# Half leads: two byte offsets inside one weight unit of an encoder trunk

## The chip, the cores and the metric

The kernel runs on one core of a Trainium2 chip, in one launch. The metric is device time in microseconds. A core has engines that run side by side: TensorE (PE in the profile, with its weight loads as PEld), VectorE (DVE), ScalarE (ACT), GpSimd (POOL) and SyncE (SP, which issues the DMAs here).

## The reference

Two layers of a hybrid encoder over 256 positions of width 1024, float32. Each layer has a token-mixing part with four branches in parallel and a feed-forward part. Cut to what matters:

```python
for l in range(DEPTH):                                   # DEPTH = 2
    h = rms_norm(x, norm_mix_pre[l])
    proj = h @ w_in[l]                                   # 1024 -> all branch inputs and gates
    (c_q, c_kv, k_rope, sc_b, sc_c, sc_x, cf_a, cf_g, gm_u, gm_v, gate_logits) = split(proj)
    y_a, y_b, y_c, y_d = ...                             # attention, short conv, Conformer conv, gMLP, each @ its w_o
    g = sigmoid(gate_logits + gate_b[l])
    merged = g0 * y_a + g1 * y_b + g2 * y_c + g3 * y_d
    x = x + rms_norm(merged @ w_out[l], norm_mix_post[l])
    h2 = rms_norm(x, norm_ffn_pre[l])
    f_g, f_u = split(h2 @ w_ffn_in[l])                   # 1024 -> 2 x 2816
    x = x + rms_norm((silu(f_g) * f_u) @ w_ffn_out[l], norm_ffn_post[l])
```

## The kernel before

All weights of a layer are cut into units of at most 128 x 2048 floats, listed by `unit_list` (line 47) in the order in which they are used. A unit is loaded by one DMA into a `raw` tile (line 341), then split (line 352) into a high part, rounded to the matmul's float32r format by ScalarE, and a low part, the rest, subtracted by VectorE. Both parts stand in one `hl` tile of 2 x 2048 + 64 floats, 65 x 256 bytes a partition; five such tiles rotate. A product of two split operands is three matmuls: high x high, high x low, low x high (`group`, line 398). The activations are split in the same way into `hth` and `htl`, each [128, 2, 8, 128]: token half, eight slices k of the 1024 input columns, and 128 tokens.

This document calls those units that hold all 1024 input rows and 256 output columns full-depth units. The code collects them in `stands` (line 329): 30 a layer, counted here from 0. Units 0 to 5 are used for the Conformer and gMLP inputs, 6 to 11 for the short convolution, 12 to 29 for the feed-forward input (columns 512 and up). `b_unit` (line 549) uses them: the weights are the stationary operand, one 128-column tile at a time, and all 256 tokens move. For each half f of the 256 output columns there are eight slices k with three matmuls each, so a unit is 48 matmuls of 128x256. The stationary tiles of the three are high, high, low of slice k; the moving ones are `hth`, `htl`, `hth`. In the `hl` tile a unit lies with a pitch of 256 columns per slice k; the high part is followed by the low part 2048 floats later.

`phase` (line 332) shifts where a unit begins in its `hl` tile: units that aren't full-depth at 0, full-depth units at 16 floats (64 bytes), and those named in `leads` at 32 floats (128 bytes). `LEADS` (line 37) picks the leads by their number among the 30: 0, 6, 9, 12 and 21. The other 25 are called ordinary units here. Of an offset only what is left modulo 256 bytes is given in this document: 128 for leads and 64 for ordinary units. The change's own words count the distance from the other side, 256 less the offset: 128 for a lead, 192 for an ordinary unit.

The order of work on each engine is planned while the program is built: a small model with a clock (lines 100 to 233) lets TensorE's matmuls advance it and issues pending ScalarE, VectorE and GpSimd work by modelled due times and ranks. Generators (attention, convolution, transposes of the hidden layer) are polled between groups of matmuls (`poll`, line 582) and put their matmuls between those of a unit, so that units 8, 10, 11 and 12 are interrupted by others. The plan goes by modelled times, not by what the chip does.

Of the kernel before, what the change touches and what calls it, by code (L numbers as in the profile page):

```python
# [15 lines left out]
ALU = mybir.AluOpType  # L16
AX = mybir.AxisListType

P = 128
L = 2  # L20
D = 1024
S = 256
T = S // P
KD = D // P
# [9 lines left out]
KG = L * NCOL  # L34
UW = 2048
ROOM = 64
LEADS = (0, 6, 9, 12, 21)
FIRST = 544

O_CQ, O_CKV, O_KR = 0, 256, 512  # L40
# [56 lines left out]
def hybrid_encoder(ctx: ExitStack, tc: tile.TileContext, wts, x_in, pos, invf, cols, rows, wst, out):  # L97
# [129 lines left out]
    def flush(ops):  # L227
        if any(o.left for o in ops):
            urge(ops)
            t = clock[0]  # L230
            while any(o.left for o in ops):
                t += 0.1
                pump(t)
# [28 lines left out]
    act, dve, pool, sp, pe = Engine(nc.scalar, "ACT", cost_act), Engine(nc.vector, "DVE", cost_dve), Engine(nc.gpsimd, "POOL", cost_pool), Engine(nc.sync, "SP", lambda *a: 0.1), Tensor()  # L262
# [14 lines left out]
    def nm(s):  # L277
        cnt[0] += 1
        return f"{s}_{cnt[0]}"
# [30 lines left out]
    def bank(s="pb", hold=False):  # L310
        return psum("pb", s, hold)
# [15 lines left out]
    NU = len(units)  # L327

    stands = [u for u in range(NU) if units[u][2] - units[u][1] == D]
    leads = {stands[k] for k in LEADS}  # L330

    def phase(i):
        u = i % NU
        return (2 if u in leads else 1 if u in stands else 0) * ROOM // 4

    class Weights:
        def __init__(self):
# [14 lines left out]
        def split(self, i):  # L352
            w = widths[i % NU]
            both = wp.tile([P, 2 * UW + ROOM], F32R, tag="hl", name=nm("hl"), bufs=B_HI)
            at0 = phase(i)
            h, lo = both[:, at0 : at0 + UW], both[:, UW + at0 : 2 * UW + at0]
            raw = self.raw.pop(i)
            step = FIRST if i == 0 else 1024
            self.parts[i] = (h, lo)
            spans = [(c, min(w, c + step)) for c in range(0, w, step)]  # L360

            def rank():
                return 0 if i <= self.n + NEAR else 3

            for c, e in spans:
                act.copy(h[:, c:e], raw[:, c:e], rank=rank)
                dve.tensor_tensor(lo[:, c:e], raw[:, c:e], h[:, c:e], op=ALU.subtract, rank=rank, then=self.more if e == w else None)

        def more(self, t=0.0):
            if self.nd < L * NU:  # L370
# [9 lines left out]
        def use(self, n):  # L380
            i = self.n
            self.n += 1
            while i not in self.parts:
                flush(list(pending["DVE"][:1]))
            w = widths[i % NU]
            return tuple(a[:, :w].rearrange("p (k n) -> p k n", n=n) for a in self.parts.pop(i))

        def free(self, n=1):
            self.nf += n
# [8 lines left out]
    def group(o, terms, first=True, last=True):  # L398
        n = len(terms)
        for i, (lh, ll, rh, rl) in enumerate(terms):  # L400
            pe.matmul(o, lh, rh, start=(first and i == 0), stop=False)
            pe.matmul(o, lh, rl, start=False, stop=False)
            pe.matmul(o, ll, rh, start=False, stop=(last and i == n - 1))
            poll()
# [42 lines left out]
    for j in range(2):  # L447
        k = slice(4 * j, 4 * j + 4)
# [46 lines left out]
    hth = cp.tile([P, T, KD, P], F32R, name="hth")  # L495
    htl = cp.tile([P, T, KD, P], F32R, name="htl")

    def pre_norm(t, g):
        h = big()
        ss = small(2)  # L500
        s1 = small(1)
        r = small(1)
        for j in range(2):
            c = slice(512 * j, 512 * (j + 1))
            act.activation(h[:, c], x[:, t, c], AF.Square, scale=D ** -0.5, accum_out=ss[:, j : j + 1], rank=FAST)
            if j == 0:
                pool.tensor_scalar(s1, ss[:, 0:1], EPS, None, op0=ALU.add, rank=FAST)
        rstd_of(r, ss[:, 1:2], s1, rank=FAST)
        if callable(g):
            g = g()  # L510
        for j in range(2):
            c = slice(512 * j, 512 * (j + 1))
            dve.scalar_tensor_tensor(h[:, c], x[:, t, c], r, g[j] if isinstance(g, list) else g[:, c], op0=ALU.mult, op1=ALU.mult, rank=FAST)

        def turn():
            for j in range(2):
                yield need(h)
                b = sbank()
                transposes(b, [h[:, 512 * j + P * k : 512 * j + P * (k + 1)] for k in range(4)])
                bv = b.rearrange("p (k n) -> p k n", n=P)  # L520
                split(hth[:, t, 4 * j : 4 * j + 4, :], htl[:, t, 4 * j : 4 * j + 4, :], bv, FAST)

        return turn()
# [25 lines left out]
    def b_unit():  # L549
        wh, wl = W.use(256)  # L550
        b = bank()
        for f in range(2):
            c = slice(f * P, (f + 1) * P)
            o = b[:, f * S : (f + 1) * S].rearrange("p (t n) -> p t n", n=P)
            group(o, [(wh[:, k, c], wl[:, k, c], hth[:, :, k, :], htl[:, :, k, :]) for k in range(KD)])
        W.free()
        return b

# [23 lines left out]
    def poll():  # L582
        nested[0] += 1
        moved = True
        while moved:
            moved = False
            for w in list(waiting):
                if ready(w):
                    w[2] = next(w[1], None)
                    if w[2] is None:  # L590
                        waiting.remove(w)
                    moved = True
                    break
        nested[0] -= 1
# [16 lines left out]
    def layer(l):  # L611
# [26 lines left out]
        def mla_tr(t, cn):  # L638
            yield need(cn)
            b = sbank()  # L640
            transposes(b, [cn[:, P * k : P * (k + 1)] for k in range(4)])
            for j in range(2):
                o = slice(t * P, (t + 1) * P)
                split(ft2(qc[j])[:, :, o], ft2(ql[j])[:, :, o], b[:, 256 * j : 256 * (j + 1)].rearrange("p (f n) -> p f n", f=2))
# [78 lines left out]
        for j in range(2):  # L723
            b = b_unit()
            th = slot(s="th")
            act.activation(th, b, AF.Tanh, scale=0.5)
            b = b_unit()
            dve.scalar_tensor_tensor(zc[j], th, 1.0, b, op0=ALU.add, op1=ALU.mult)

        def split_op(name, j, src):  # L730
            hi, lo = slot(F32R, name + "h"), slot(F32R, name + "l")
            split(hi, lo, src)
            ops[name][j] = (ft2(hi), ft2(lo))
# [41 lines left out]
        for j in range(2):  # L775
            b = b_unit()
            u = slot(s="gu")
            act.activation(u, b, AF.Gelu_apprx_tanh)
            ug.append(u)
# [433 lines left out]
```

## Time and profile before

| | |
|---|---|
| time, median of 3 runs | 947.82 us (947.7 to 948.02) |
| the profiled execution | 948.06 us |
| its span, first to last instruction | 946.3 us |
| PE busy | 936.9 us, 5888 matmuls |
| DVE, ACT, POOL busy | 670.5, 476.5, 49.0 us |
| mean granted TensorE clock | 0.998 |
| DMA | 179.10 MB, mean 189 GB/s |

The profile is of one execution, whose time stands in the second line. Busy time counts an engine's instructions from start to end; matmuls overlap in the pipeline and their ends are modelled, so the start times of the timeline are the surer reading of TensorE's pace. In timeline rows that merge two matmuls, the start is that of the first. The third matmul of one group and the first of the next both read `hth` and are merged into one row; the middle matmul reads `htl` and has a row of its own in each group.

### The profile page before, as it was taken

The page shows a single profiled execution, that of the slowest core. Times are in us where ns is not written, and L with a number is a line of the kernel's source. Part 1 is how long each engine was busy: PE and PEld are TensorE (multiplying, and loading weights), DVE is VectorE, ACT ScalarE, POOL GpSimd, SP SyncE. Part 2 cuts the span into 40 slices and gives each one's busy share as a digit, 9 for nine tenths or more (in the row PEclk, how much of TensorE's full clock was granted, in tenths as well). Part 3 has the DMA queues.
Part 4 walks back from the last instruction along what each step waited for, and adds up shares of the span by engine and source line. Part 5 has one row for each costly group of instructions (what it writes and reads, how often), then busy time and mean ns, then how long its engine had stood idle before and what let it go on. Part 6 is the DMA issues. An engine that isn't in the chain of part 4 may idle for free.

```text
span 946.3 us, 14540 instructions
## 1 busy us (share of the span) xinstructions
PE 936.9 (99%) x5888; PEld 843.1 (89%) x5888; DVE 670.5 (71%) x1000; ACT 476.5 (50%) x729; POOL 49.0 (5%) x95
## 2 busy tenths in 40 slices
PE   8999999999999999999999999999999999999997
PEld 7899988888888999998899999888888889999885
DVE  6879888898857755554387888788887675555532
ACT  7666745446436644444275656544454454544421
POOL 2200000000002000000041000000000110000000
PEclk9999999999999999999999999999999999999999
DMA  9845354565845655564268244455567366555601
GB/s 349 292 172 178 116 185 149 178 213 189 318 166 178 222 181 201 198 228 178 90 244 291 69 164 164 150 178 195 202 239 265 117 216 235 210 181 185 239 1 44
DMA packets 29875, 179.10 MB, mean 189 GB/s; under 512 B 3824, under 2 KB 3952, under 8 KB 10352
## 3 DMA queue, kind: packets, MB, share of 16 engines
q1 hardware_dynamic: 29664, 178.17, 53.4%
q8 instruction: 46, 0.75, 0.3%
q14 instruction: 21, 0.17, 0.0%
q10 hardware_dynamic: 144, 0.00, 0.0%
HBM read 177.11 MB, written 1.05 MB: 188 GB/s over the span
## 4 chain that ended last, share of the span: by engine, by line
PE 98%; DMA 1%; issue 1%; SPq 0%; ACT 0%; DVE 0%; DVEq 0%; POOLq 0%; POOL 0%
PE pb L256 79%; PE acc L256 12%; PE psd L260 4%; PE psd L256 2%; PE av L256 1%; DMA x<-in_x_dram 1%; SPq L317 0%; ACT h L176 0%; DVE x L176 0%; DVEq L1209 0%; POOLq L1209 0%; ACT hl L176 0%; POOL c L176 0%
## 5 line engine op out<-in xcount | busy, mean ns | idle before, releaser
L176 ACT CAST hl<-raw 128x1024 fp32r<-128x1024 f32 (+4 forms) x321 | 322.2, 1035 | 301.9 <-issue 169.0
L176 DVE TENSOR_TENSOR hl<-raw,hl 128x1024 fp32r<-128x1024 f32 (+4 forms) x321 | 376.7, 1201 | 119.3 <-ACT hl L176 119.3
L256 PE MATMUL pb<-hth,hl 128*128 128x256 f32 x1920 | 334.1, 278 | 0.0
L256 PEld LDWEIGHTS pb<-hth,hl 128*128 128x128 f32 x1920 | 291.6, 188 | 0.4
L256 PE MATMUL pb<-htl,hl 128*128 128x256 f32 x960 | 266.3, 277 | 0.0
L256 PE MATMUL pb<-hl,hth 128*128 128x512 f32 (+1 forms) x832 | 239.5, 379 | 0.4 <-ACT hl L176 0.4
L256 PEld LDWEIGHTS pb<-htl,hl 128*128 128x128 f32 x960 | 180.4, 188 | 0.4
L256 PEld LDWEIGHTS pb<-hl,hth 128*128 128x128 f32 x832 | 147.3, 188 | 26.9 <-ACT hl L176 0.6
L256 PE MATMUL pb<-hl,htl 128*128 128x512 f32 (+1 forms) x416 | 147.4, 375 | 0.2 <-DVE htl L176 0.2
L256 PE MATMUL acc<-hl,fh 128*128 128x512 f32 x352 | 108.5, 389 | 0.0
L176 DVE SCALAR_TENSOR_TENSOR yc<-zc,hcol,yc 128x241 f32<-128x241 f32 (+14 forms) x240 | 97.8, 470 | 0.0
L256 PEld LDWEIGHTS pb<-hl,htl 128*128 128x128 f32 x416 | 74.8, 188 | 14.5 <-DVE htl L176 0.4
L256 PEld LDWEIGHTS acc<-hl,fh 128*128 128x128 f32 x352 | 65.9, 188 | 13.5
L256 PE MATMUL acc<-hl,fl 128*128 128x512 f32 x176 | 68.5, 389 | 0.0
L256 PE MATMUL pb<-hl,mh 128*128 128x512 f32 x128 | 40.0, 394 | 0.0
L256 PEld LDWEIGHTS acc<-hl,fl 128*128 128x128 f32 x176 | 33.0, 188 | 6.8
L176 POOL TENSOR_SCALAR c<-c 128x1 f32<-128x1 f32 (+1 forms) x20 | 12.8, 638 | 503.0 <-ACT sq L176 455.6
L176 DVE TENSOR_TENSOR f<-f,pb 128x512 f32<-128x512 f32 x22 | 15.1, 687 | 30.3 <-PE pb L256 30.3
L176 ACT COPY pt<-psd 128x512 f32<-128x512 f32 x16 | 9.4, 585 | 39.7 <-PE psd L260 39.7
L256 PEld LDWEIGHTS pb<-hl,mh 128*128 128x128 f32 x128 | 23.6, 188 | 4.6
L176 DVE TENSOR_TENSOR h<-acc,gain 128x512 f32<-128x512 f32 x8 | 5.4, 690 | 28.6 <-ACT sq L176 28.5
L256 PE MATMUL pb<-hl,ml 128*128 128x512 f32 x64 | 25.0, 390 | 0.0
(149 smaller groups left out, 837.8 us busy)
## 6 DMA issues: line engine op xcount, KB each, us to landing
raw<-in_wts_dram SPq DMA_DIRECT2D x152, 1024.0 KB, 4.8
brow<-in_rows_dram SPq DMA_DIRECT2D x24, 256.0 KB, 6.0
gain<-in_rows_dram SPq DMA_DIRECT2D x7, 512.0 KB, 5.9
raw<-in_wts_dram SPq DMA_DIRECT2D x3, 816.0 KB, 4.3
raw<-in_wts_dram SPq DMA_DIRECT2D x2, 768.0 KB, 6.7
raw<-in_wts_dram SPq DMA_DIRECT2D x2, 544.0 KB, 5.8
out_dram<-x SPq DMA_DIRECT2D x4, 256.0 KB, 2.1
raw<-in_wts_dram SPq DMA_DIRECT2D x3, 272.0 KB, 4.7
```

What stands on the lines that cost most here:

```text
L176: o.emit = lambda: f(*a, **k)
L256: nc.tensor.matmul(out, lhsT, rhs, **k)
L260: nc.tensor.transpose(out=out, in_=in_, identity=identity)
```

## The change

Placement: `phase` is replaced by `places`, which gives for each unit the places of the first and second 1024 elements of its high part and of its low part in the `hl` tile. For an ordinary unit these are high at 16 and 1040, low at 2064 and 3088 floats (64 bytes modulo 256, as before). For a lead the first 1024 elements are at 2080 (high) and 3104 (low), that is 128 bytes modulo 256, and the second 1024 at 16 and 1040, that is 64 bytes.

Layout: the full-depth units are stored in memory half by half: all eight slices of output columns 0 to 127 first, then those of columns 128 to 255, so that the first 1024 elements are the first half f and the pitch of a slice is 128 columns instead of 256. `b_unit` takes the tiles accordingly. DMAs, copies and subtractions keep their number and sizes.

Leads: 21 is no longer one; 0, 6, 9 and 12 remain.

```diff
--- before.py
+++ after.py
@@ -34,7 +34,7 @@
 KG = L * NCOL
 UW = 2048
 ROOM = 64
-LEADS = (0, 6, 9, 12, 21)
+LEADS = (0, 6, 9, 12)
 FIRST = 544
 
 O_CQ, O_CKV, O_KR = 0, 256, 512
@@ -329,9 +329,11 @@
     stands = [u for u in range(NU) if units[u][2] - units[u][1] == D]
     leads = {stands[k] for k in LEADS}
 
-    def phase(i):
+    def places(i):
         u = i % NU
-        return (2 if u in leads else 1 if u in stands else 0) * ROOM // 4
+        if u in leads:
+            return (2080, 16), (3104, 1040)
+        return ((16, 1040), (2064, 3088)) if u in stands else ((0, 1024), (2048, 3072))
 
     class Weights:
         def __init__(self):
@@ -352,19 +354,18 @@
         def split(self, i):
             w = widths[i % NU]
             both = wp.tile([P, 2 * UW + ROOM], F32R, tag="hl", name=nm("hl"), bufs=B_HI)
-            at0 = phase(i)
-            h, lo = both[:, at0 : at0 + UW], both[:, UW + at0 : 2 * UW + at0]
             raw = self.raw.pop(i)
             step = FIRST if i == 0 else 1024
-            self.parts[i] = (h, lo)
+            self.parts[i] = both
             spans = [(c, min(w, c + step)) for c in range(0, w, step)]
 
             def rank():
                 return 0 if i <= self.n + NEAR else 3
 
             for c, e in spans:
-                act.copy(h[:, c:e], raw[:, c:e], rank=rank)
-                dve.tensor_tensor(lo[:, c:e], raw[:, c:e], h[:, c:e], op=ALU.subtract, rank=rank, then=self.more if e == w else None)
+                hi, lo = (both[:, p[c // 1024] + c % 1024 :][:, : e - c] for p in places(i))
+                act.copy(hi, raw[:, c:e], rank=rank)
+                dve.tensor_tensor(lo, raw[:, c:e], hi, op=ALU.subtract, rank=rank, then=self.more if e == w else None)
 
         def more(self, t=0.0):
             if self.nd < L * NU:
@@ -383,7 +384,10 @@
             while i not in self.parts:
                 flush(list(pending["DVE"][:1]))
             w = widths[i % NU]
-            return tuple(a[:, :w].rearrange("p (k n) -> p k n", n=n) for a in self.parts.pop(i))
+            both = self.parts.pop(i)
+            if i % NU in stands:
+                return tuple(tuple(both[:, o : o + 1024].rearrange("p (k n) -> p k n", n=P) for o in p) for p in places(i))
+            return tuple(both[:, o : o + w].rearrange("p (k n) -> p k n", n=n) for o, _ in places(i))
 
         def free(self, n=1):
             self.nf += n
@@ -550,9 +554,8 @@
         wh, wl = W.use(256)
         b = bank()
         for f in range(2):
-            c = slice(f * P, (f + 1) * P)
             o = b[:, f * S : (f + 1) * S].rearrange("p (t n) -> p t n", n=P)
-            group(o, [(wh[:, k, c], wl[:, k, c], hth[:, :, k, :], htl[:, :, k, :]) for k in range(KD)])
+            group(o, [(wh[f][:, k, :], wl[f][:, k, :], hth[:, :, k, :], htl[:, :, k, :]) for k in range(KD)])
         W.free()
         return b
 
@@ -1170,7 +1173,10 @@
     for l in range(L):
         for name, r0, r1, cols in units:
             w = src[name][l][r0:r1, cols]
-            parts.append(w.reshape(-1, P, w.shape[1]).transpose(1, 0, 2).reshape(-1))
+            w = w.reshape(-1, P, w.shape[1])
+            if r1 - r0 == D:
+                w = w.reshape(KD, P, -1, P).transpose(2, 0, 1, 3).reshape(-1, P, P)
+            parts.append(w.transpose(1, 0, 2).reshape(-1))
     wts = np.concatenate(parts)
 
     def colmajor(v):
```

## Rows read from the trace of the kernel before

**Rows 1.** The page: span, PE's busy time, granted clock in 40 slices.

```profile
span 946.3 us, 14540 instructions
...
PE 936.9 (99%) x5888; PEld 843.1 (89%) x5888; DVE 670.5 (71%) x1000; ACT 476.5 (50%) x729; POOL 49.0 (5%) x95
...
PEclk9999999999999999999999999999999999999999
```

**Rows 2.** The page, part 4: the chain that ended last, by engine.

```profile
PE 98%; DMA 1%; issue 1%; SPq 0%; ACT 0%; DVE 0%; DVEq 0%; POOLq 0%; POOL 0%
```

**Rows 3.** The page, part 5: split copies and 128x256 matmuls (out<-in xcount | busy, mean ns).

```profile
L176 ACT CAST hl<-raw 128x1024 fp32r<-128x1024 f32 (+4 forms) x321 | 322.2, 1035 | 301.9 <-issue 169.0
L176 DVE TENSOR_TENSOR hl<-raw,hl 128x1024 fp32r<-128x1024 f32 (+4 forms) x321 | 376.7, 1201 | 119.3 <-ACT hl L176 119.3
L256 PE MATMUL pb<-hth,hl 128*128 128x256 f32 x1920 | 334.1, 278 | 0.0
...
L256 PE MATMUL pb<-htl,hl 128*128 128x256 f32 x960 | 266.3, 277 | 0.0
```

**Rows 4.** Waits of PE: line, releaser: us in total, times, longest.

```profile
PE pb L256 <- ACT hl L176: 0.4, 1, 0.4
PE pb L256 <- DVE htl L176: 0.2, 1, 0.2
```

**Rows 5.** Timeline of PE (start us, us, what), layer 1, units 6 and 7.

```profile
80.32 0.28 PE L256 MATMUL pb<-htl,hl 128*128 128x256 f32 x1
...
83.20 0.28 PE L256 MATMUL pb<-htl,hl 128*128 128x256 f32 x1
...
86.09 0.28 PE L256 MATMUL pb<-htl,hl 128*128 128x256 f32 x1
...
88.81 0.28 PE L256 MATMUL pb<-htl,hl 128*128 128x256 f32 x1
```

**Rows 6.** Timeline of PE, layer 1, units 20 to 22.

```profile
362.95 0.28 PE L256 MATMUL pb<-htl,hl 128*128 128x256 f32 x1
...
363.29 0.28 PE L256 MATMUL pb<-htl,hl 128*128 128x256 f32 x1
...
363.63 0.28 PE L256 MATMUL pb<-htl,hl 128*128 128x256 f32 x1
...
365.67 0.28 PE L256 MATMUL pb<-htl,hl 128*128 128x256 f32 x1
...
366.02 0.29 PE L256 MATMUL pb<-htl,hl 128*128 128x256 f32 x1
...
368.52 0.28 PE L256 MATMUL pb<-htl,hl 128*128 128x256 f32 x1
...
371.37 0.28 PE L256 MATMUL pb<-htl,hl 128*128 128x256 f32 x1
```

**Rows 7.** Timeline of PE, layer 1, units 12 and 13, and the last of unit 29.

```profile
317.66 0.60 PE L260 MATMUL psd<-ident,f 128*128 128x128 f32 x4
...
322.13 0.28 PE L256 MATMUL pb<-htl,hl 128*128 128x256 f32 x1
...
324.87 0.28 PE L256 MATMUL pb<-htl,hl 128*128 128x256 f32 x1
...
414.55 0.28 PE L256 MATMUL pb<-htl,hl 128*128 128x256 f32 x1
```

**Rows 8.** Timeline of PE, layer 1, units 10 and 11, behind attention work.

```profile
109.07 0.28 PE L256 MATMUL pb<-htl,hl 128*128 128x256 f32 x1
...
111.79 0.28 PE L256 MATMUL pb<-htl,hl 128*128 128x256 f32 x1
...
118.44 0.28 PE L256 MATMUL pb<-htl,hl 128*128 128x256 f32 x1
...
121.26 0.28 PE L256 MATMUL pb<-htl,hl 128*128 128x256 f32 x1
```

## The prediction

> **What bounds the kernel now.** I began with the page's head and its busy shares: TensorE is busy for 936.9 of 946.3 us, at a granted clock in the top tenth in every slice, so it runs at the 2.4 GHz level throughout [rows 1]. The chain that ended last is 98% PE [rows 2]. The waits of PE on the prepared weights come to 0.4 + 0.2 us in the whole run [rows 4]. So a nanosecond saved between two matmuls is a nanosecond of the run, and nothing else can give much. The next thing to read is therefore not who waits, but at what pace matmuls follow each other.
>
> Half of all matmuls belong to the 60 full-depth units: 1920 + 960 = 2880 of 128x256, 48 a unit (two halves of eight groups of three) [rows 3]. The mean of 278 ns in that row hides the pace, since matmuls overlap; the timeline gives it. In each group of three the middle matmul is the only one that reads `htl`, so the start of one `htl` row to the next is one group, and eight groups later is one half unit. Three paces stand there:
> - Ordinary units: 0.34 us a group, 2.72 us a half. Unit 7 of layer 1, 86.09 to 88.81 [rows 5]; unit 20, three successive rows 0.34 apart, and 362.95 to 365.67 [rows 6].
> - Leads: 0.355 to 0.36 us a group. Unit 6 takes 2.88 and 2.89 us for its halves [rows 5], unit 21 takes 2.85 and 2.85 [rows 6]. Of the ten leads three have the 2.88 of unit 6 (units 0 and 6 of layer 1, unit 6 of layer 2), the other seven the 2.85 of unit 21.
> - Some stretches of ordinary units that begin behind other matmuls: 0.353 us a group. Unit 11 of layer 1, 118.44 to 121.26, has 2.82 for eight [rows 8]. Units 10 and 11 of layer 2 are the same.
>
> So an ordinary unit has a fast and a slow pace, 13 ns a group apart, and keeps the one it is in: from 324.87 to 414.55 the feed-forward stage has 263 groups, which at 0.34 make 89.42, and the other 0.26 us are the lead at unit 21 [rows 7]. The trace says what sets the pace: behind a lead, the ordinary unit is fast after about a group (all ten leads); behind an interruption without a lead it is a lottery (unit 10 of layer 1 came out fast, 109.07 to 111.79, the three others slow) [rows 8]. A lead is slower than either pace of an ordinary unit, and what it buys is the fast pace after it. Why a byte offset does this no row shows; I use it as an observed rule.
>
> **The change, part by part.**
>
> *Half a lead instead of a whole one (units 0, 6, 9, 12, both layers: eight leads).* The first 24 matmuls keep offset 128 and their cost. The other 24 get the ordinary offset and, if the fast pace comes, 2.72 us. The three slow leads save 2.88 - 2.72 = 0.16 us each, 0.48; the other five save 2.85 - 2.72 = 0.13 each, 0.65. Together 1.13 us. The switch itself is paid today at the border of the units and then in the middle of one: 322.13 to 324.87 is 2.74, so it costs 0.02 or less [rows 7], and cancels.
>
> *Lead 21 removed.* Units 13 to 29 then have one offset. 365.67 to 371.37 is 5.70 us where two fast halves are 5.44: 0.26 us, with about 0.01 more in the first group after it, so 0.53 for both layers. This needs that the fast pace holds without a second lead for 17 units; today it holds for eight and a half before unit 21 and eight after, with no drift in the rows.
>
> *Weights laid out half by half (256-column pitch to 128).* Copies and subtractions stay at two pieces of 1024 each a unit, 1.04 and 1.20 us [rows 3], the same bytes per DMA, the same order on SP, and no wait is added; each piece is needed no earlier than before (the second 12 matmuls later), so beside PE waits of 0.6 us in all it gives nothing and costs nothing. If this cover were gone (DVE later than PE), 2.4 us of subtraction a unit would still fit into 5.44. What the trace doesn't show is the pace when successive stationary tiles are 512 bytes apart instead of 1024. The ends: every group at the lead's 0.36 costs 60 x 16 x 0.02 = 19 us; every group at 0.34, the fastest that any row of this shape has, would give another 1.13 us in the leads' first halves and 0.6 in the three slow stretches. I take zero, far nearer to the second: today the moving tile steps by 512 bytes per k and the stationary one by 1024, so their offset alternates with even and odd k, and successive groups are still equally 0.34 apart [rows 6]; the buffers are 65 x 256 bytes long, so offsets of 256 alternate from unit to unit as well, and all ordinary units of that stage have the pace. The row nearest to the new case says that only the offset below 256 counts.
>
> *Sum.* 1.13 + 0.53 = 1.66 us, all on the path. The profiled execution took 948.06 us (span 946.3 and 1.8 around it, untouched): 946.40. It lies 0.24 above the median of 947.82, for which the same sum gives 946.16, say **946.2 us, 0.17% less**. About 0.2% (1.9 us) is what a measurement of this kernel can tell from no change, so this counts as "same", though close to the edge.
>
> **The rivals.**
>
> *1. The half lead at unit 12 fails to bring the fast pace (slower).* Today a lead has 48 matmuls behind an interruption, or at unit 12, where four transposes break in at 317.66, 15 before them and 33 after [rows 7]. With half a lead only nine stand between those transposes and the switch. For it to work: unit 21 is at the lead's pace from its first group (365.67 to 366.02 is 0.35) [rows 6], so nine should do. Against: none of the ten switches came so soon after a restart, and a wrong moment costs as unit 11 does. Price: half of unit 12 and 17 units are 280 groups at 2.82/8 - 0.34 = 0.0125 to 0.0133 us, 3.6 us a layer: both layers 953.4, one layer 949.8 (beyond +0.2%). It decides against the change as soon as it happens in one layer. Both layers have the same order of work, so both is likelier: 0.09, against 0.02 for one. The same failure at unit 0 costs 88 groups, 1.2 us, so 947.4 for one layer: 0.03.
>
> *2. The lead's extra time belongs to its place, not its offset (no change).* Being the first of a stage, it would keep its 2.85 in any layout: 947.8. For it: four of five leads do follow other work. Against: unit 21 follows ordinary units without a gap, is slow from its first group to its last, and unit 22 is fast again [rows 6]. 0.04.
> [...]
>
> *3. The fast pace is lost in the long stage without lead 21 (slower).* From unit 21 on, nine units are 144 groups x 0.013 = 1.9 us a layer: 946.2 + 3.8 = 950.0 (two layers). Against: no loss in any row so far, and PE waits for no weights there. 0.03.
>
> *4. The restarts in units 10 and 11 fall differently (faster or nothing).* The change moves the work before them by 0.1 to 0.2 us each, and the state in which the attention's matmuls interrupt. Each of the four stretches has 15 groups, 0.2 us. All fast would give 0.6: 945.6; the one fast one lost gives 946.4. Below 945.9 needs two of the three slow ones to turn. 0.17.
>
> **How the numbers follow.** Forecast 0.62; rival 4 on the fast side 0.17; rival 1 0.14 (0.03 of it within 0.2%); rival 2 0.04; rival 3 0.03. Faster by over 0.2% (below 945.9): 0.17, and 0.02 for the measurement's own spread (947.7 to 948.02 before), 0.19. Slower (above 949.7): 0.09 + 0.02 + 0.03 = 0.14. Same: 0.67. The range runs from all restarts fast, 945.5, to the loss at unit 0 in one layer, 947.5, and leaves out rivals 2, 3 and the large part of 1.
>
> **What would show it.** In the timeline, second halves of units 0, 6, 9 and 12 at 2.72 to 2.74 us, first halves unchanged at 2.85 to 2.89, unit 21 at 2.72 a half, 0.34 a group up to the end of the stage; span 944.6. Wrong if groups of 0.353 follow unit 12 (rival 1), if second halves stay at 2.85 (rival 2), if 0.34 turns to 0.353 in mid-stage (rival 3), or if ordinary units are no longer at 0.34 at all (the layout).

## The result: slower, 953.95 us, and the profile after

The changed kernel takes 953.95 us (953.48 to 954.75) where the kernel before took 947.92 beside it: ratio 1.0064, 95% interval 1.0052 to 1.0076. The forecast of 946.2 and its range (945.5 to 947.5) are missed; the time is that of the first rival on both layers (953.4).

The page of the changed kernel (span; busy us of PE and the other engines):

```profile
span 953.0 us, 14540 instructions
...
PE 944.1 (99%) x5888; PEld 850.8 (89%) x5888; DVE 670.7 (70%) x1000; ACT 476.7 (50%) x729; POOL 47.5 (5%) x95
```

PE's busy time has grown with the span, by 7.2 and 6.7 us, at as many matmuls as before [rows 1]; the granted clock is 0.998 as before. The waits of PE on weights are still next to nothing (releaser: us in total, times, longest), as in [rows 4]:

```profile
PE pb L256 <- DVE htl L176: 0.5, 2, 0.4
```

So the matmuls follow each other more slowly, and the timeline says where. Unit 6 of layer 1 (start us, us, what; `htl` rows are one group of three apart, eight groups make a half):

```profile
80.74 0.28 PE L256 MATMUL pb<-htl,hl 128*128 128x256 f32 x1
...
83.62 0.28 PE L256 MATMUL pb<-htl,hl 128*128 128x256 f32 x1
...
86.34 0.28 PE L256 MATMUL pb<-htl,hl 128*128 128x256 f32 x1
```

The half lead does what it should here: 2.88 us for the first half, 2.72 for the second, which took 2.89 in [rows 5]. The same holds for unit 0 in both layers, unit 6 of layer 2 and unit 9 of layer 1. In the feed-forward stage of layer 1 four transposes break into unit 12. The first row is theirs; the others are the first group of unit 12's second half, the first groups of unit 13's two halves, and the last group of unit 29:

```profile
318.01 0.60 PE L260 MATMUL psd<-ident,f 128*128 128x128 f32 x4
...
319.63 0.28 PE L256 MATMUL pb<-htl,hl 128*128 128x256 f32 x1
...
322.46 0.28 PE L256 MATMUL pb<-htl,hl 128*128 128x256 f32 x1
...
325.28 0.28 PE L256 MATMUL pb<-htl,hl 128*128 128x256 f32 x1
...
418.21 0.28 PE L256 MATMUL pb<-htl,hl 128*128 128x256 f32 x1
```

From 325.28 to 418.21 there are 263 groups in 92.93 us, 0.3533 a group, where [rows 7] have 89.68 with a lead in it. Nothing changes on the way; units 20 and 21, where the lead of before stood, are like all others:

```profile
364.86 0.28 PE L256 MATMUL pb<-htl,hl 128*128 128x256 f32 x1
...
367.68 0.28 PE L256 MATMUL pb<-htl,hl 128*128 128x256 f32 x1
...
370.51 0.28 PE L256 MATMUL pb<-htl,hl 128*128 128x256 f32 x1
...
373.34 0.28 PE L256 MATMUL pb<-htl,hl 128*128 128x256 f32 x1
```

2.82 to 2.83 a half against 2.72 for an ordinary half and 2.85 for a lead in [rows 6]. Layer 2 is the same: 92.93 us over the same 263 groups (793.55 to 886.48). The stage is at the slow pace from the switch in unit 12 to its end, on both layers.

The sum closes. The forecast was -1.66 us. 280 slow groups (half of unit 12 and 17 units) at 0.3533 - 0.34 = 0.0133 us are 3.73 a layer, 7.47 for both; unit 9 of layer 2 switched into the slow pace as well (second half 2.83 instead of 2.72, 0.11) and unit 10 of layer 1 restarted slow (15 groups, 0.20). Together +6.1 us, against 6.03 by the medians. The profiled span grew by 6.7; the other 0.6 us come before unit 0 begins (36.48 against 35.91 for its first `htl` row), in the start-up.

### The profile page after: what moved, and what is told of

Read it like the earlier page. It is cut to its first block, busy times and chain, and to the rows that moved or that the text cites. A ratio compares the mean times of both kernels' runs of the same rounds, so it can differ in the third digit from the quotient of the medians.

```text
span 953.0 us, 14540 instructions
## 1 busy us (share of the span) xinstructions
PE 944.1 (99%) x5888; PEld 850.8 (89%) x5888; DVE 670.7 (70%) x1000; ACT 476.7 (50%) x729; POOL 47.5 (5%) x95
## 4 chain that ended last, share of the span: by engine, by line
PE 97%; DMA 1%; issue 1%; ACT 0%; DVE 0%; DVEq 0%; POOLq 0%; SPq 0%; POOL 0%
PE pb L256 78%; PE acc L256 12%; PE psd L260 3%; PE psd L256 2%; PE av L256 1%; DMA raw<-in_wts_dram 1%; DMA cos<-in_cols_dram 0%; ACT hl L176 0%; ACT hth L176 0%; DVE x L176 0%; DVEq L1215 0%; POOLq L1215 0%; SPq L317 0%; DVE htl L176 0%; ACT cn L176 0%
## 5 line engine op out<-in xcount | busy, mean ns | idle before, releaser
L256 PE MATMUL pb<-hth,hl 128*128 128x256 f32 x1920 | 340.2, 281 | 0.0
L256 PEld LDWEIGHTS pb<-htl,hl 128*128 128x128 f32 x960 | 182.7, 190 | 0.4
```

Of the source, the lines that this page charges most:

```text
L256: nc.tensor.matmul(out, lhsT, rhs, **k)
```

## The experiments

The 10 ns of the timeline's rows hide what follows; the trace's start times have 1 ns. Behind the transposes of unit 12 the lead's start-to-start times repeat with a period of five: about 122, 120, 119, 115, 118 ns, mean 118.7. "The 122" below is that place of this period. The leads of unit 6, and of unit 0 in layer 1, repeat with a period of three instead, about 117, 120, 123 ns. Three theories were set against each other. *Moment*: what decides is the place in this pattern on which the offset changes; on the 122 the ordinary tiles fall into the slow pace, anywhere else into the fast one. *Length*: nine matmuls behind an interruption are too few for a lead to work. *Layout*: a switch inside a unit, or the 128-column pitch, doesn't work in this stage.

All kernels but one are the changed kernel with a number of groups of three for each lead (16 is a whole lead), and pieces of the split cut at the switch. Here is the edit of the first of them, cut to what matters; each piece is its first and last element and the places of its high and low part:

```diff
-LEADS = (0, 6, 9, 12)
+LEADS = {0: 8, 6: 8, 9: 8, 12: 7}
...
     def places(i):
...
+        g = P * leads.get(u, 0)
...
+        r = UW - g
+        h, lo = 32 + 2 * r, 32 + 2 * r + g
+        if g <= 1280:
+            return (0, g, h, lo), (g, UW, 16, 16 + r)
```

TensorE's order of work is the same in all of them, apart from the last run, where a few of attention's and other small matmuls move by a group; the transposes of unit 12 stay where they are.

**How long unit 12's lead is.** Four kernels, `12: 7`, `12: 9`, `12: 13` and `12: 16`.

> The changed kernel with one edit: at unit 12 of both layers the first 7 groups of three stand at offset 128 instead of the first 8, so the switch comes 6 matmuls after the four transposes instead of 9. Theory 'moment': behind those transposes the lead's start-to-start times repeat with a period of five (about 122, 120, 119, 115, 118 ns), and a switch that falls on the 122 leads into the slow pace, any other into the fast one. The 6th matmul after the restart stands at 119, so the feed-forward stage runs at 0.340 us a group: 946.5 us, range 946.0 to 947.2. Rival 'length': 9 matmuls after an interruption were too few for a lead to work, so 6 are too few as well: 0.353 a group, 953.5 to 954.5. Rival 'layout' (a switch inside a unit, or the 128-column pitch, doesn't work in this stage): 953.5 to 954.5 too.

> As the run with 7 groups, but with 9 groups at offset 128 at unit 12: the switch comes 12 matmuls after the transposes, at the place of 115 ns in the pattern. 'Moment': fast, 0.340 us a group in units 13 to 29, 946.5 us (946.0 to 947.2). 'Length': 12 instead of 9 may or may not do, so 946.5 or 954. 'Layout': slow, 953.5 to 954.5.

> As the run with 7 groups, but with 13 groups at offset 128 at unit 12: the switch comes 24 matmuls after the transposes, again on the 122 of the pattern. 'Moment': slow, although the lead is more than half as long again as in the changed kernel: 0.353 us a group in units 13 to 29, 954.0 us (953.4 to 954.6). 'Length': 24 matmuls are plenty, fast, 946.8 us. 'Layout': slow. The unit's weights are split in three pieces instead of two, one more ScalarE copy and VectorE subtraction a layer, beside TensorE's work.

> As the run with 7 groups, but unit 12 is a whole lead again (16 groups at offset 128); the other half leads, the layout and the missing lead at 21 stay. The switch comes 33 matmuls after the transposes, at the place of 118 ns. 'Moment' and 'length': fast, 946.8 us (946.3 to 947.4), about 0.25 above the fast runs with 7 and 9 groups. 'Layout' (128-column pitch): slow, 954. If lead 21 is what keeps the stage fast, the pace turns to 0.353 somewhere between units 13 and 29: 950 or more.

Measured, in this order: 946.11 us, ratio to the kernel before 0.9985 (0.9975 to 0.9994); 946.22, 0.9984 (0.9975 to 0.9993); 953.66, 1.0064 (1.0047 to 1.0081); 946.43, 0.9989 (0.9979 to 0.9998). A shorter lead works and a longer one, with 13 groups, doesn't. The timeline with 7 groups, first groups of unit 12's second half and of unit 13, last group of unit 29:

```profile
318.46 0.28 PE L256 MATMUL pb<-htl,hl 128*128 128x256 f32 x1
...
321.18 0.28 PE L256 MATMUL pb<-htl,hl 128*128 128x256 f32 x1
...
413.32 0.28 PE L256 MATMUL pb<-htl,hl 128*128 128x256 f32 x1
```

and with 13 groups:

```profile
318.72 0.28 PE L256 MATMUL pb<-htl,hl 128*128 128x256 f32 x1
...
324.38 0.28 PE L256 MATMUL pb<-htl,hl 128*128 128x256 f32 x1
...
417.31 0.28 PE L256 MATMUL pb<-htl,hl 128*128 128x256 f32 x1
```

With 7 groups the 279 groups to the end take 94.86 us, 0.340 each. With 13 the lead still covers five groups of the second half, and the 263 groups behind 324.38 take 92.93, 0.3533 each, as in the changed kernel. With 9 and 16 groups the same 263 take 89.42:

```profile
323.83 0.28 PE L256 MATMUL pb<-htl,hl 128*128 128x256 f32 x1
...
413.25 0.28 PE L256 MATMUL pb<-htl,hl 128*128 128x256 f32 x1
```

```profile
323.87 0.28 PE L256 MATMUL pb<-htl,hl 128*128 128x256 f32 x1
...
413.29 0.28 PE L256 MATMUL pb<-htl,hl 128*128 128x256 f32 x1
```

The start-to-start times in ns, layer 1, from the restart behind the transposes; the bar stands where the first tile at the ordinary offset begins:

```
 7 groups,  6 matmuls: 202 117 118 122 120 116 | 114 113 114 113 113 114
 8 groups,  9 matmuls: 202 117 118 122 120 119 115 118 117 | 118 118 117 118 118 118
 9 groups, 12 matmuls: 202 117 118 122 120 119 115 118 121 120 120 116 | 123 118 113 114 113 113
13 groups, 24 matmuls: 202 117 118 122 120 ... 122 120 119 115 117 118 | 118 118 117 118 118 118
16 groups, 33 matmuls: 203 116 119 121 120 ... 122 120 119 115 118 | 117 123 118 113 114 113
```

With 8 and 13 groups the last interval would have been the 122 and came out as 117 or 118; the flat 118 behind it is the slow pace. *Length* would have the 6 matmuls slow and the 24 fast, *layout* would have all of them slow; both are excluded.

**The same test without an interruption.** Two kernels, `12: 7` with `21: 5` or `21: 6`.

> The kernel with 7 groups of lead at unit 12 (946.1 us, fast to the end), with a lead of 5 groups put back at unit 21, in the middle of the fast stretch, where nothing interrupts. Entered from the fast pace a lead begins 114, 120, 112, 117 and then repeats 122, 120, 119, 115, 118; its 15th matmul falls on the 122. 'Moment': the switch there throws the stage into the slow pace, 0.353 from unit 21 to 29, 139 groups x 0.0133 = 1.9 us a layer: 949.9 us. 'Any lead is good for the pace, if long enough': 15 uninterrupted matmuls keep it fast, 946.3.

> As the run with 5 groups of lead at unit 21, but with 6: the switch comes after 18 matmuls, on the 115 of the pattern. 'Moment': the stage stays fast, 946.3 us. If it is the lead's length, or having a lead there at all, that spoils the pace, this one is slow as well: 949.9.

Measured: 950.29 us, 1.0026 (1.0016 to 1.0037), and 946.67, 0.9986 (0.9976 to 0.9995). One group of three decides on 3.6 us. First groups of unit 20's second half, of unit 21's two halves and of unit 22, and for the first the end of the stage; with 5 groups:

```profile
362.44 0.28 PE L256 MATMUL pb<-htl,hl 128*128 128x256 f32 x1
...
365.16 0.28 PE L256 MATMUL pb<-htl,hl 128*128 128x256 f32 x1
...
368.00 0.28 PE L256 MATMUL pb<-htl,hl 128*128 128x256 f32 x1
...
370.82 0.28 PE L256 MATMUL pb<-htl,hl 128*128 128x256 f32 x1
...
415.70 0.28 PE L256 MATMUL pb<-htl,hl 128*128 128x256 f32 x1
```

with 6 groups:

```profile
362.60 0.28 PE L256 MATMUL pb<-htl,hl 128*128 128x256 f32 x1
...
365.32 0.28 PE L256 MATMUL pb<-htl,hl 128*128 128x256 f32 x1
...
368.15 0.28 PE L256 MATMUL pb<-htl,hl 128*128 128x256 f32 x1
...
370.87 0.28 PE L256 MATMUL pb<-htl,hl 128*128 128x256 f32 x1
...
414.05 0.28 PE L256 MATMUL pb<-htl,hl 128*128 128x256 f32 x1
```

Both arrive at the fast pace (2.72). Behind unit 22's first group 127 groups remain: 44.88 us with 5 (0.3534 each), 43.18 with 6 (0.340). The start-to-start times of unit 21 in ns, layer 1, the bar as above:

```
5 groups, 15 matmuls: 113 120 112 117 123 120 120 115 117 122 120 119 115 117 118 | 117 119 117 118 118 118
6 groups, 18 matmuls: 113 120 113 116 124 120 119 115 117 122 120 119 115 118 121 120 120 116 | 123 118 113 114 113 113
```

With 5 groups the 15th interval stands where the next 122 was due. A lead that ends on the 122 throws a fast stretch into the slow pace.

**No lead at unit 12**, `{0: 8, 6: 8, 9: 8}`.

> The changed kernel without any lead at unit 12 (half leads at 0, 6 and 9 stay): the feed-forward stage begins at offset 64 and is interrupted by the four transposes at that offset. What a lead is for: if the pace behind an interruption is left to chance, 0.353 us a group behind the transposes as in three of four stretches of units 10 and 11 of the kernel before, 953.5 to 954.5 us; if the stage would come out fast without a lead, 946.0, and the half lead of the changed kernel itself did the damage.

Measured: 953.35 us, 1.0062 (1.0047 to 1.0078).

```profile
318.41 0.28 PE L256 MATMUL pb<-htl,hl 128*128 128x256 f32 x1
...
321.24 0.28 PE L256 MATMUL pb<-htl,hl 128*128 128x256 f32 x1
...
416.99 0.28 PE L256 MATMUL pb<-htl,hl 128*128 128x256 f32 x1
```

279 groups in 98.58 us, 0.3533: without a lead the stage is slow from its first matmuls on (117 and 118 ns even before the transposes). So a lead is needed there. The half lead of the changed kernel gave the same 98.58 us for these groups, in both layers, and its own first half took longer (3.31 us in unit 12 against 3.27 without a lead).

**The two other parts alone.** The kernel before without the lead at 21 (whole leads, old layout), and the new layout with five whole leads (`{0: 16, 6: 16, 9: 16, 12: 16, 21: 16}`).

```diff
-LEADS = (0, 6, 9, 12, 21)
+LEADS = (0, 6, 9, 12)
```

> The kernel before with LEADS = (0, 6, 9, 12): whole leads, old layout, only the lead at 21 gone. 'Moment' and my prediction: the fast pace holds from unit 13 to 29 without it, 0.340 us a group to the end of the stage, 0.53 us less than the kernel before. If lead 21 is needed to keep the pace: 0.353 from some unit on, up to 3.8 us more.

> The changed kernel's layout (half by half, 128-column pitch), but five whole leads as before (0, 6, 9, 12, 21). If the layout is neutral, as predicted: the time of the kernel before within 0.2%, ordinary units at 0.340 us a group, leads at 0.356 to 0.360. If the pitch costs or gives something: another pace in all 60 units, 1 us for each nanosecond a group.

Measured: 947.55 us, 0.9998 (0.9989 to 1.0008), and 947.94, 0.9999 (0.9990 to 1.0009). The intervals are too wide for 0.53 us; the timeline shows it. First group of unit 13's second half to the last of unit 29, without the lead at 21:

```profile
326.92 0.28 PE L256 MATMUL pb<-htl,hl 128*128 128x256 f32 x1
...
416.34 0.28 PE L256 MATMUL pb<-htl,hl 128*128 128x256 f32 x1
```

89.42 us, 263 times 0.340: the fast pace holds to the end, and the 0.26 us of [rows 7] are gone, in layer 2 too. With the new layout and five leads:

```profile
324.89 0.28 PE L256 MATMUL pb<-htl,hl 128*128 128x256 f32 x1
...
365.70 0.28 PE L256 MATMUL pb<-htl,hl 128*128 128x256 f32 x1
...
371.39 0.28 PE L256 MATMUL pb<-htl,hl 128*128 128x256 f32 x1
...
414.58 0.28 PE L256 MATMUL pb<-htl,hl 128*128 128x256 f32 x1
```

89.69 us and 5.69 for the lead, as before [rows 6, 7]: the layout is neutral.

**Leads as short as the pattern allows**, `{0: 3, 6: 2, 9: 3, 12: 7}`.

> The kernel with 7 groups of lead at unit 12, with the other leads cut too: 3 groups at units 0 and 9, 2 at unit 6 (the first piece of these units is split at the switch, one copy and one subtraction more a unit). 'Moment': at unit 0 the 9th matmul of the four starts seen so far stands at 115 to 118, at unit 6 every switch has worked, unit 9 may fall on the 122 in one run of five (0.5 us): 946.1 - 0.58 = 945.5 us. If so short leads don't work: up to 1.3 us more a layer for unit 0, 0.6 for unit 6.

Measured: 945.18 us, 0.9974 (0.9964 to 0.9984): faster than both kernels. Unit 0 of layer 1, first groups of its halves and of unit 1:

```profile
35.65 0.28 PE L256 MATMUL pb<-htl,hl 128*128 128x256 f32 x1
...
38.44 0.28 PE L256 MATMUL pb<-htl,hl 128*128 128x256 f32 x1
...
41.16 0.28 PE L256 MATMUL pb<-htl,hl 128*128 128x256 f32 x1
```

The half with the lead takes 2.79 us instead of 2.89. At unit 0 the switch was not on the places that the expectation names: in layer 1 it stood on the longest interval of a period of three, in layer 2 on the 119, and both came out fast. In this run attention's matmuls moved to right in front of unit 9, so its lead, too, ended nine matmuls behind an interruption; it ended on the 119, beside the 122, and both layers went fast.

## Why the prediction was wrong, point by point

- *What bounds the kernel.* Right: no wait came up, and the whole difference is the pace of the 128x256 matmuls.
- *Half leads, 1.13 us.* The switch inside a unit costs at most 0.01 us and gives 2.72 to 2.73 us where the fast pace comes; it came at units 0 and 6 of both layers and unit 9 of layer 1. At unit 12 of both layers and unit 9 of layer 2 it didn't.
- *Lead 21, 0.53 us.* Right, shown alone: 89.42 instead of 89.68 a layer. (Eight units stood before that lead, not eight and a half.)
- *Layout, zero.* Right, shown alone.
- *Rival 1.* It named the place (unit 12, nine matmuls behind the transposes), the price (3.6 us a layer; 3.73 measured) and that both layers would go together, and had a chance of 0.09 for both. The step that failed is the rule "behind a lead, the ordinary unit is fast after about a group (all ten leads)", and with it the sentence that talked the rival down: "unit 21 is at the lead's pace from its first group …, so nine should do". I took a lead as something that has worked once its pace is there. What the runs showed instead is that the place of the switch in the lead's period decides: behind the transposes 6 matmuls do, 9 don't, 12 do, 24 don't, 33 do, and both that fail end on the 122. The stage then runs at 0.3533 us a group instead of 0.340. The count that I used as a worry (no switch so soon after a restart) was not the quantity either: at unit 9 of the last run the fast pace followed a lead of nine matmuls right behind an interruption. The rule was also read from fewer leads than it says: behind unit 9 only three matmuls follow before attention breaks in, so eight of the ten could be judged.
- *What could have been read before.* Seven leads of the kernel before have the period of five, and none of them ended on the 122: at unit 12 the 33rd interval behind the transposes is the 118. The other three have the period of three. The start times in ns had all this; I read the trace in groups, where 122, 120 and 119 become 0.35 and 0.36. This trace doesn't show that the 122 is the bad place. It does show that a switch after nine matmuls stands on a place that no switch of before had tried, and the forecast should have given rival 1 far more than 0.09.
- *Rival 3.* Didn't happen (run without lead 21). *Rival 2* didn't either: second halves went to 2.72. (What was said for it is off by one lead: unit 9 follows three matmuls of unit 8, so three of the five leads directly follow other work.) *Rival 4*: unit 10 of layer 1 restarted slow, 0.2 us lost, within the range. Its fast side, 0.17, needed unit 11 to turn in at least one layer, and unit 11 restarted slow in all 24 stretches of the twelve profiles; unit 10 was fast in 17 of 24.

Over the twelve profiles there are 102 changes from offset 128 to 64. Six are interrupted by other matmuls too early to be judged. Of the other 96, nine stood on the 122 of the period of five and all became slow; 50 stood on other places of that period and all became fast. The last 37 belong to leads with the period of three (units 0 and 6 as named above, and in one profile unit 0 of layer 2). All of these ended on its longest interval, and all became fast, so a long interval alone is not what makes the pace slow; the two other places of that period were not tried.

The runs with 5 and 6 groups, and with 7, 8, 9 and 13, show the place as a cause: the edit is the number of groups alone, and each outcome but that of the changed kernel, with 8, was forecast from the place. The parts of the unit move in the `hl` tile with that number, by multiples of 512 bytes. That this is not the cause can be seen at unit 9: its half lead of 8 groups lies at the same places in eight of the profiles, and of its 16 switches the three on the 122 became slow, the other 13 fast. Which place unit 9 meets changes from one profile to the next, and so do the last start-to-start times before it; no run shows what sets them. Why the 122 is the bad place stays open: no run here looks below the start times, and none moves the other operand.

## What to carry to other kernels

Where a matmul stream has several stable paces, read start-to-start times of single matmuls in ns before costing an edit: a mean over groups hides the pattern in which the edit lands. An edit that moves a switch should be tried at two or three neighbouring positions, since one group of three decided on 3.6 us at unit 21 and on about 7.5 us at unit 12 here (ratio 1.0064 with 8 groups, 0.9985 with 7). A shorter lead is worth having (945.18 against 947.8 us) only when its end is placed by that pattern and not by the border of a unit half.

## What the runs showed of the hardware

- The same 128x256 matmul at the full granted clock follows its predecessor after 113.3, 117.8, 118.7 or 120 ns on average, by the byte offset of the stationary tiles modulo 256 and by what went before. The first two are paces of offset 64, and each held for all 263 groups behind unit 13's first half, until the end of the stage (89.42 us without a lead at 21, 92.93 in the changed kernel); the other two are those of offset 128. No third offset was tried.
- Six matmuls at another offset behind an interruption can put a stage on the fast pace to its end (unit 12 with 7 groups: 94.86 us for 279 groups). A stretch that starts at offset 64 behind other work can stay slow to its end (no lead at unit 12: 98.58 us for the same groups).
- 24 matmuls at that offset can leave the stage slow, when the change of offset falls on the 122 (13 groups: 92.93 us for 263 groups, against 89.42 with 9).
- The pitch between successive stationary tiles (1024 or 512 bytes) made no difference: 89.69 against 89.68 us.
